# Two SBUF pools of a two-block transformer kernel taken from the other end of the memory

## The chip, the core and the metric

One NeuronCore of a Trainium2 chip runs the whole program in one launch. The metric is device time in microseconds (us): the median of the runs of a kernel. Engines are named as in the profile: PE is TensorE, PEld its weight loads, DVE is VectorE, ACT is ScalarE, POOL is GpSimd, SP the queue that issues most DMAs.

## What is computed

256 tokens of width 1024 pass through two float32 blocks. Cut to what matters:

```python
for l in range(2):                                   # first block
    x = x + 0.5 * swiglu(rms_norm(x, ffn1_norm[l]), ffn1_w1[l], ffn1_w2[l])
    x = x + hybrid_mixer(rms_norm(x, mix_norm[l]), ...)   # LRU, latent attention, convolution
    x = x + 0.5 * swiglu(rms_norm(x, ffn2_norm[l]), ffn2_w1[l], ffn2_w2[l])
x = rms_norm(x, final_norm)
h = x                                                # second block
h = h + dilated_mixer(rmsnorm(h, a_norm[0]), ...)    # three dilated attentions, merged
h = h + swiglu_2(rmsnorm(h, ffn_norm[0]), ...)
h = h + forgetting_mixer(rmsnorm(h, b_norm[0]), ...)
h = h + swiglu_2(rmsnorm(h, ffn_norm[1]), ...)
return rmsnorm(h, final_norm_2)
```

`swiglu(x, w1, w2)` is `(silu(g) * u) @ w2` with `g, u` the halves of `x @ w1`; the hidden width is 2816.

## The kernel before

Every large product is made of three reduced-precision (fp32r) products. An operand A is kept as two halves, AH (A rounded to fp32r) and AL (the rest), and A times W is AH·WH + AH·WL + AL·WH. So each tile product is three matmuls, lines 342, 343 and 344 in `tm` (tokens on the output partitions) or 359, 360 and 361 in `fm` (features on them).

In `tm` the activation half, 128x128, is the stationary operand, loaded before each matmul, and the weight half, 128x512 in most products, is the moving operand, streamed through. In `fm` it is the other way round, with 256 moving columns.

Weights come in slabs of 128x1024 float32 (`slab`, lines 323 to 325): SP loads one into a `raw` buffer, ACT rounds it to `H`, and DVE makes `L` by subtraction. There are five `raw` buffers, three `H` and three `L`, all in pool `wp`. Small long-lived tiles of the norms (sums of squares, scales, the scratch `scr`) are in pool `sp`.

Activation halves lie in different tiles. `XH`, `XL` (pool `xp`, with the residual `x`) hold the normed input of a stage; every first product of a stage reads them. The hidden halves `HH`, `HL` of the feed-forward layers, `XN`, `XP` (the input in two other token orders, dilated mixer), `OH`, `OL` (attention outputs), and in the hybrid mixer `fr`, `oH`, `oL`, `ycH`, `ycL` are in a pool that `scoped` opens for a stage and closes after it. The stages follow each other: feed-forward, hybrid mixer, feed-forward, twice; then dilated mixer, feed-forward, forgetting mixer, feed-forward.

The pools are stacked in the order in which they are opened, from the low end of each SBUF partition unless `side="right"` is given. Within a pool tiles follow each other, each padded to 32 bytes. The order of instructions on each engine, and what each waits for, comes from the recording order and a scheduler.

Of the kernel before, what the change touches and what calls it, by code (L numbers as in the profile page):

```python
# [19 lines left out]
S = 256  # L20
# [9 lines left out]
HD = 64  # L30
# [167 lines left out]
class K:  # L198
    def __init__(self, ctx, tc, A):
        self.ctx, self.tc, self.nc, self.A = ctx, tc, tc.nc, A  # L200
        self.n = 0
        P = lambda n, b=1, **k: ctx.enter_context(tc.tile_pool(name=n, bufs=b, **k))
        self.const = P("const")
        self.xp = P("xp")
        self.wp = P("wp", 3)
        self.sp = P("sp", 2)
        pp = P("pp", space=bass.MemoryType.PSUM)
        self.bank = pp.tile([128, 8, 512], F32, name="bank")
        self.psum("wide")
# [117 lines left out]
        return v(H), v(L)  # L327

    def tm(self, name, l, chunks, XH, XL):
        """Token-major products of several column chunks, their k-groups interleaved."""  # L330
        nc = self.nc
        ws = [WSPEC[name][1][c][1] for c in chunks]
        kt = WSPEC[name][0] // 128
        ps = [[self.mm()[:, :w] for _ in range(2)] for w in ws]
        for (k0, n), ci in itertools.product(_kgroups(name, ws[0]), range(len(chunks))):
            H, L = self.slab(name, l, chunks[ci], k0, n)
            for t in range(2):
                for k in range(n):
                    a, z = k0 + k == 0, k0 + k == kt - 1
                    xh, xl = (X[:, k0 + k, 128 * t:128 * t + 128] for X in (XH, XL))  # L340
                    p = ps[ci][t]
                    nc.tensor.matmul(p, xh, H[:, k, :], start=a, stop=False)  # L342
                    nc.tensor.matmul(p, xh, L[:, k, :], start=False, stop=False)  # L343
                    nc.tensor.matmul(p, xl, H[:, k, :], start=False, stop=z)  # L344
        return ps

    def fm(self, name, l, chunks, XH, XL):
        """Feature-major products of 256-column chunks, [128, 2, S] each, their k-groups interleaved."""
        nc = self.nc
        kt = WSPEC[name][0] // 128  # L350
        ps = [self.mm2() for _ in chunks]
        for k0, n in _kgroups(name, 256):
            for chunk, p in zip(chunks, ps):
                H, L = self.slab(name, l, chunk, k0, n)
                for k in range(n):
                    a, z = k0 + k == 0, k0 + k == kt - 1
                    for j in range(2):
                        wh, wl = H[:, k, 128 * j:128 * j + 128], L[:, k, 128 * j:128 * j + 128]
                        nc.tensor.matmul(p[:, j, :], wh, XH[:, k0 + k, :], start=a, stop=False)  # L359
                        nc.tensor.matmul(p[:, j, :], wl, XH[:, k0 + k, :], start=False, stop=False)  # L360
                        nc.tensor.matmul(p[:, j, :], wh, XL[:, k0 + k, :], start=False, stop=z)  # L361
        return ps

    def transpose_split(self, src, k0, n, OH, OL, ko, gain=None, const=None, dil=1):
        """Token-major src[:, t, columns] to feature-major halves OH/OL[:, ko.., :];
        the tokens by residue modulo dil first."""
        nc = self.nc
        for k in range(0, n, 2):
            m = min(2, n - k)
            p = self.pt()[:, :m * S].rearrange("p (k s) -> p k s", k=m)  # L370
            for j in range(m):
                for t in range(2):
                    nc.tensor.transpose(p[:, j, 128 * t:128 * t + 128],  # L373
                                        src[:, t, 128 * (k0 + k + j):128 * (k0 + k + j + 1)], self.ident)
            if gain is None:
                h, lo = OH[:, ko + k:ko + k + m, :], OL[:, ko + k:ko + k + m, :]
                if const is None:
                    nc.scalar.copy(h, p)
                    nc.vector.tensor_sub(lo, p, h.bitcast(F32))
                else:  # L380
                    nc.scalar.activation(h, p, AF.Copy, scale=const)
                    nc.vector.scalar_tensor_tensor(lo, p, const, h.bitcast(F32), op0=OP.mult, op1=OP.subtract)
            else:
                for j in range(m):
                    g = gain[:, ko + k + j:ko + k + j + 1]
                    h, lo, pj = OH[:, ko + k + j, :], OL[:, ko + k + j, :], p[:, j, :]
                    if dil > 1:
                        h, lo = (z.rearrange("p (c i) -> p c i", c=dil) for z in (h, lo))
                        pj = pj.rearrange("p (i c) -> p c i", c=dil)
                    nc.scalar.activation(h, pj, AF.Copy, scale=g)  # L390
                    nc.vector.scalar_tensor_tensor(lo, pj, g, h.bitcast(F32), op0=OP.mult, op1=OP.subtract)  # L391
# [31 lines left out]
        return r  # L423

    def norm_twice(self, row, g1, g2, dil):
        """x becomes its norm by g1; the operands and scales are those of the norm of that by g2,
        the operands' tokens by residue modulo dil first."""
        nc, x = self.nc, self.x
        es, p = self.scoped("twice")
        gb = p.tile([128, D], F32, name="gb")  # L430
# [66 lines left out]
        es.close()  # L497

    def log1p_exp(self, p, e, n, tag):
        """log(1 + e) for e in (0, 1], by 2 artanh(e / (2 + e))."""  # L500
        nc = self.nc
        z = p.tile([128, n], F32, name=tag + "z")
        z2 = p.tile([128, n], F32, name=tag + "y")
        q = p.tile([128, n], F32, name=tag + "q")
        nc.vector.tensor_scalar(z2, e, 2.0, None, op0=OP.add)
        nc.vector.reciprocal(z2, z2)
        nc.vector.tensor_mul(z, e, z2)
        nc.vector.tensor_mul(z2, z, z)
        nc.vector.tensor_scalar(q, z2, 1.0 / 17, None, op0=OP.mult)
        for c in (15, 13, 11, 9, 7, 5, 3):  # L510
            nc.vector.scalar_tensor_tensor(q, q, 1.0 / c, z2, op0=OP.add, op1=OP.mult)
        nc.vector.scalar_tensor_tensor(q, q, 1.0, z, op0=OP.add, op1=OP.mult)
        nc.vector.tensor_scalar(q, q, 2.0, None, op0=OP.mult)
        return q

    def rope(self, tmp, dst, src, n, c0, w):
        """Rotates the last-dim halves (w each) of src [128, 2, n, 2w] into dst."""
        nc = self.nc
        m = 2 * n * w
        tmp = [tmp[:, m * i:m * i + m].rearrange("p (t n w) -> p t n w", t=2, n=n) for i in range(4)]  # L520
        shape = [128, 2, n, w]
        cs = self.cos[:, :, None, c0:c0 + w].to_broadcast(shape)
        sn = self.sin[:, :, None, c0:c0 + w].to_broadcast(shape)
        x1, x2 = src[:, :, :, :w], src[:, :, :, w:2 * w]
        nc.vector.tensor_mul(tmp[0], x1, cs)
        nc.vector.tensor_mul(tmp[1], x2, sn)
        nc.vector.tensor_mul(tmp[2], x2, cs)
        nc.vector.tensor_mul(tmp[3], x1, sn)
        nc.vector.tensor_sub(dst[:, :, :, :w], tmp[0], tmp[1])
        nc.vector.tensor_add(dst[:, :, :, w:2 * w], tmp[2], tmp[3])  # L530

    def attend(self, ap, qk, mask, v, nm, den, o, act, local):
        """One head: qk holds its queries and keys, [w, 2 * S]; leaves P V in o[t] (PSUM).
        Blocks of scores: (queries 1, keys 0 | 1), (queries 0, keys 0), or only the diagonal ones;
        the causal mask leaves the first block as it is."""
        nc = self.nc
        n = 2 if local else 3
        keys = (0, 1) if local else (0, 1, 0)
# [24 lines left out]
                nc.tensor.matmul(o[t], PT[:, 128 * i:128 * i + 128], v[:, keys[i], :], start=i == a, stop=i == b - 1)  # L563

    def heads(self, ap, which, q, k, w, mask, v, store, act=False, local=False, stats=None):
        """Attention of heads a pair (from those of `which`) at a time; q, k: [128, 2, n, w] token-major, v: [128, 2, n, HD]."""
        nc = self.nc
        for h in which:
            ops = []
# [28 lines left out]
            store(h, o, nm, den)  # L598

    def normalized(self, ap, OH, OL, ko):  # L600
        """Keeps a pair of heads' normalized output as a feature tile of OH/OL."""
        nc = self.nc

        def store(h, o, nm, den):
# [5 lines left out]
        return store  # L610

    def bcast(self, dst, r):
        """Per-token column r [128, 2] to a row, the same on every partition."""
        nc = self.nc
        p = self.pt()[:, :S]
        for t in range(2):
# [305 lines left out]
    def dilated(self):  # L922
# [26 lines left out]
            nc.vector.tensor_scalar(one, r8[:, 2, 0:1], 1.0, 1.0, op0=OP.min, op1=OP.max)  # L949

        def copy(i, dst, src):
            """Scaled by one, which holds the copy back until the scales are there."""
            if i:
                nc.vector.tensor_scalar(dst, src, one, None, op0=OP.mult)
            else:
                nc.scalar.activation(dst, src, AF.Copy, scale=one)
# [179 lines left out]
```

## Time and profile before

| what | value |
|---|---|
| three runs, median (lowest to highest) | 2091.37 us (2090.86 to 2091.70) |
| span of the profiled execution | 2086.7 us |
| median of the runs less that span | 4.7 us |
| PE busy, of the span | 2052.3 us, 98% |
| chain that ended last, PE's share | 90% |
| DVE, ACT busy | 1304.4 us, 1088.6 us |
| DMA, mean over the span | 171 GB/s |

The profiled execution has no time of its own beside its span; what lies around the span is taken as the 4.7 us of the third row. A matmul's duration in the trace contains its way through the array and overlaps its neighbours, so how fast PE goes is read from the distance of two starts, not from durations.

### The profile page before, as it was taken

The numbers are of one execution on the slowest core, as the hardware profiler recorded it, in microseconds if no ns is written. First come the engines' busy times: TensorE is split into PE (matmuls) and PEld (weight loads), VectorE is DVE, ScalarE is ACT, GpSimd is POOL, SyncE is SP. The second block draws the span as 40 slices with busy tenths as digits, with TensorE's granted clock in tenths as the row PEclk, the third lists the DMA queues.
The fourth block names the chain that finished last, engine by engine and source line by source line (L and its number), as shares of the span: only waits on it lengthen the run. The fifth ranks groups of instructions, "written<-read, shape, count | busy, mean of one in ns | idle before, by whom it ended". The sixth has DMA issues, their size and how long they took to land.

```text
span 2086.7 us, 27788 instructions
## 1 busy us (share of the span) xinstructions
PE 2052.3 (98%) x10542; PEld 1709.8 (82%) x10542; DVE 1304.4 (63%) x2042; ACT 1088.6 (52%) x1681; POOL 19.7 (1%) x31
## 2 busy tenths in 40 slices
PE   8999999999999999999999999889999999999998
PEld 7888988788878888988788877667778888888886
DVE  4555999855555556998755565445775554555554
ACT  5444685554444445684554457445555544555443
POOL 0000000000000000000000000000000000000000
PEclk9999999999999999999999999999999999999999
DMA  6666554556565666454555554445436655436653
GB/s 218 183 204 193 180 172 153 171 185 185 181 188 181 190 179 201 158 181 152 191 182 184 181 171 137 141 145 177 131 111 183 187 179 160 130 103 192 183 181 120
DMA packets 100301, 356.00 MB, mean 171 GB/s; under 512 B 11176, under 2 KB 12216, under 8 KB 100168
## 3 DMA queue, kind: packets, MB, share of 16 engines
q1 hardware_dynamic: 98920, 351.69, 53.8%
q0 software_dynamic: 528, 1.26, 0.3%
q8 instruction: 82, 1.34, 0.3%
q10 hardware_dynamic: 720, 1.29, 0.2%
q14 instruction: 51, 0.42, 0.1%
HBM read 350.59 MB, written 3.21 MB: 170 GB/s over the span
## 4 chain that ended last, share of the span: by engine, by line
PE 90%; issue 3%; DMA 3%; ACT 2%; DVE 1%; POOL 0%; ACTq 0%; SPq 0%; POOLq 0%; DVEq 0%
PE bank L343 25%; PE bank L342 25%; PE bank L344 25%; PE bank L373 2%; PE bank L563 2%; PE bank L544 2%; PE bank L558 1%; PE bank L361 1%; PE bank L359 1%; PE bank L360 1%; DMA T<-X 1%; PE bank L584 1%; DVE L L325 1%; ACT H L324 1%; DMA x<-in_x 1%
## 5 line engine op out<-in xcount | busy, mean ns | idle before, releaser
L325 DVE TENSOR_TENSOR L<-raw,H 128x1024 fp32r<-128x1024 f32 (+1 forms) x653 | 791.9, 1214 | 628.3 <-ACT H L324 626.3
L324 ACT CAST H<-raw 128x1024 fp32r<-128x1024 f32 (+1 forms) x653 | 681.0, 1043 | 841.6 <-PE bank L344 782.4
L343 PE MATMUL bank<-L,XH 128*128 128x512 f32 (+3 forms) x1680 | 633.0, 377 | 6.7 <-DVE L L325 6.7
L342 PE MATMUL bank<-H,XH 128*128 128x512 f32 (+3 forms) x1680 | 638.0, 380 | 0.1
L344 PE MATMUL bank<-H,XL 128*128 128x512 f32 (+3 forms) x1680 | 629.5, 377 | 0.5 <-DVE XL L391 0.4
L343 PEld LDWEIGHTS bank<-L,XH 128*128 128x128 f32 x1680 | 318.3, 189 | 60.4 <-DVE L L325 8.3
L342 PEld LDWEIGHTS bank<-H,XH 128*128 128x128 f32 x1680 | 318.3, 189 | 55.3 <-ACT XH L390 2.0
L344 PEld LDWEIGHTS bank<-H,XL 128*128 128x128 f32 x1680 | 317.4, 189 | 56.2 <-DVE XL L391 2.6
L342 PE MATMUL bank<-H,HH 128*128 128x512 f32 x528 | 209.2, 396 | 0.0
L343 PE MATMUL bank<-L,HH 128*128 128x512 f32 x528 | 208.2, 394 | 0.0
L344 PE MATMUL bank<-H,HL 128*128 128x512 f32 x528 | 208.2, 394 | 0.0
L342 PEld LDWEIGHTS bank<-H,HH 128*128 128x128 f32 x528 | 99.2, 188 | 23.9
L344 PEld LDWEIGHTS bank<-H,HL 128*128 128x128 f32 x528 | 98.8, 187 | 24.2
L343 PEld LDWEIGHTS bank<-L,HH 128*128 128x128 f32 x528 | 98.9, 187 | 23.8
L787 DVE SCALAR_TENSOR_TENSOR acc<-cpad,cvec,acc 128x256 f32<-128x256 f32 x240 | 103.9, 476 | 0.0
L360 PE MATMUL bank<-XH,L 128*128 128x256 f32 x256 | 72.0, 283 | 0.0
L359 PE MATMUL bank<-XH,H 128*128 128x256 f32 x256 | 71.8, 285 | 0.1
L361 PE MATMUL bank<-XL,H 128*128 128x256 f32 x256 | 71.0, 284 | 0.1
L563 PEld LDWEIGHTS bank<-v,PT 128*128 128x128 f32 x416 | 54.0, 191 | 6.6 <-DVE PT L560 2.7
L563 PE MATMUL bank<-v,PT 128*128 128x64 f32 x416 | 55.3, 268 | 0.2 <-DVE PT L560 0.2
L486 DVE SCALAR_TENSOR_TENSOR h<-bank,r,t 128x512 f32<-128x512 f32 (+1 forms) x72 | 48.2, 699 | 8.3 <-PE bank L344 8.2
L485 ACT ACTIVATE t<-bank,r 128x512 f32<-128x512 f32 (+1 forms) x72 | 47.4, 659 | 10.1 <-PE bank L344 10.1
(329 smaller groups left out, 2178.7 us busy)
## 6 DMA issues: line engine op xcount, KB each, us to landing
raw<-in_ffn_w SPq DMA_DIRECT2D x264, 512.0 KB, 3.5
raw<-in_ffn_w_gu SPq DMA_DIRECT2D x88, 512.0 KB, 3.6
raw<-in_w_in SPq DMA_DIRECT2D x80, 512.0 KB, 3.5
raw<-in_a_w_in SPq DMA_DIRECT2D x72, 512.0 KB, 3.6
raw<-in_ffn_w_down SPq DMA_DIRECT2D x44, 512.0 KB, 3.6
raw<-in_b_w_in SPq DMA_DIRECT2D x24, 512.0 KB, 3.4
raw<-in_w_out SPq DMA_DIRECT2D x16, 512.0 KB, 3.5
raw<-in_mla_w_o SPq DMA_DIRECT2D x8, 512.0 KB
```

Of the source, the lines that this page charges most:

```text
L324: nc.scalar.copy(H[:, :nw], raw[:, :nw])
L325: nc.vector.tensor_sub(L[:, :nw], raw[:, :nw], H[:, :nw].bitcast(F32))
L342: nc.tensor.matmul(p, xh, H[:, k, :], start=a, stop=False)
L343: nc.tensor.matmul(p, xh, L[:, k, :], start=False, stop=False)
L344: nc.tensor.matmul(p, xl, H[:, k, :], start=False, stop=z)
L359: nc.tensor.matmul(p[:, j, :], wh, XH[:, k0 + k, :], start=a, stop=False)
L360: nc.tensor.matmul(p[:, j, :], wl, XH[:, k0 + k, :], start=False, stop=False)
L361: nc.tensor.matmul(p[:, j, :], wh, XL[:, k0 + k, :], start=False, stop=z)
L485: nc.scalar.activation(tt[:, t, :w], pg[t], AF.Silu, scale=r[:, t:t + 1])
L486: nc.vector.scalar_tensor_tensor(h[:, t, :w], pu[t], r[:, t:t + 1], tt[:, t, :w], op0=OP.mult, op1=OP.mult)
L563: nc.tensor.matmul(o[t], PT[:, 128 * i:128 * i + 128], v[:, keys[i], :], start=i == a, stop=i == b - 1)
L787: nc.vector.scalar_tensor_tensor(acc[:, c], cpad[:, c, tap:tap + S], dww[:, tap, c:c + 1], acc[:, c], op0=OP.mult, op1=OP.add)
```

## The change

The pools `wp` and `sp` are opened with `side="right"`, so they are stacked down from the high end of a partition. The pools of the stages, opened later at the low end, then begin where `XL` ends. The diff also blanks the docstrings of a dozen functions; these make no instruction.

```diff
         self.const = P("const")
         self.xp = P("xp")
-        self.wp = P("wp", 3)
-        self.sp = P("sp", 2)
+        self.wp = P("wp", 3, side="right")
+        self.sp = P("sp", 2, side="right")
         pp = P("pp", space=bass.MemoryType.PSUM)
...
     def tm(self, name, l, chunks, XH, XL):
-        """Token-major products of several column chunks, their k-groups interleaved."""
+
```

On all five engines the changed program has the same instructions in the same order, with the same waits, as the one before: no row of the order differs. All that differs is the place of tiles in a partition. Start addresses in bytes, from the two built programs, and what is left of them modulo 128:

| tile | before | mod 128 | after | mod 128 |
|---|---|---|---|---|
| `x`, `XH`, `XL` | 24064, 32256, 40448 | 0 | the same | 0 |
| `raw` (first of five, 4096 apart) | 48640 | 0 | 184288 | 96 |
| `H` (first of three, 4096 apart) | 69120 | 0 | 204768 | 96 |
| `L` (first of three, 4096 apart) | 81408 | 0 | 217056 | 96 |
| tiles of `sp` | 93696 to 96287 | | 181664 to 184255 | |
| start of a stage's pool | 96320 | 64 | 48640 | 0 |
| `HH`, `HL` (five of six layers) | 96320, 118848 | 64 | 48640, 71168 | 0 |
| `HH`, `HL` (last layer) | 108608, 131136 | 64 | 60928, 83456 | 0 |
| `XN0`, `XP0` | 112704, 129088 | 64 | 65024, 81408 | 0 |
| `fr`, `oH`, `ycH` | 122688, 168000, 184384 | 64 | 75008, 120320, 136704 | 0 |
| `OH` (dilated) | 96320 | 64 | 48640 | 0 |
| `OH`, `OL` (forgetting) | 96672, 104864 | 32 | 48992, 57184 | 96 |

Slices that a matmul reads of `XH`, `HH` and the like begin at multiples of 512 bytes in the tile, those of `H` and `L` in 512-column products at multiples of 2048, so the last column holds for each of them.

## Rows read from the trace of the kernel before

**Rows 1.** The page, parts 1 and 4: busy time by engine; chain that ended last.
```profile
PE 2052.3 (98%) x10542; PEld 1709.8 (82%) x10542; DVE 1304.4 (63%) x2042; ACT 1088.6 (52%) x1681; POOL 19.7 (1%) x31
...
PE 90%; issue 3%; DMA 3%; ACT 2%; DVE 1%; POOL 0%; ACTq 0%; SPq 0%; POOLq 0%; DVEq 0%
```

**Rows 2.** Instruction groups by shape, PE: line, out<-stationary pair, count | busy us, mean ns.
```profile
L342 PE MATMUL bank<-H,XH 128*128 128x512 f32 x1408 | 558.6, 397 | 0.1
...
L342 PE MATMUL bank<-H,HH 128*128 128x512 f32 x528 | 209.2, 396 | 0.0
...
L360 PE MATMUL bank<-XH,L 128*128 128x256 f32 x256 | 72.0, 283 | 0.0
...
L342 PE MATMUL bank<-H,XH 128*128 128x256 f32 x192 | 54.8, 285 | 0.0
...
L342 PE MATMUL bank<-H,XP 128*128 128x512 f32 x96 | 40.2, 419 | 0.0
...
L342 PE MATMUL bank<-H,XN 128*128 128x512 f32 x96 | 39.8, 414 | 0.0
...
L342 PE MATMUL bank<-H,OH 128*128 128x512 f32 x64 | 26.9, 420 | 0.2 <-ACT OH L378 0.2
...
L342 PE MATMUL bank<-H,fr 128*128 128x512 f32 x48 | 19.4, 404 | 0.0
...
L342 PE MATMUL bank<-H,ycH 128*128 128x512 f32 x32 | 12.8, 401 | 0.3 <-DVE ta L843 0.3
L342 PE MATMUL bank<-H,oH 128*128 128x512 f32 x32 | 12.7, 396 | 0.0
```

**Rows 3.** Timeline of PE (start us, duration us), feed-forward first product, stationary XH, XL.
```profile
439.80 0.39 PE L344 MATMUL bank<-H,XL 128*128 128x512 f32 x1
...
447.28 0.39 PE L344 MATMUL bank<-H,XL 128*128 128x512 f32 x1
```

**Rows 4.** The same view, feed-forward second product, stationary HH, HL.
```profile
760.15 0.39 PE L342 MATMUL bank<-H,HH 128*128 128x512 f32 x1
...
767.85 0.39 PE L342 MATMUL bank<-H,HH 128*128 128x512 f32 x1
```

**Rows 5.** The same view, forgetting mixer's output product, stationary OH, OL.
```profile
1878.73 0.39 PE L342 MATMUL bank<-H,OH 128*128 128x512 f32 x1
...
1886.43 0.39 PE L342 MATMUL bank<-H,OH 128*128 128x512 f32 x1
```

**Rows 6.** The same view, hybrid mixer, where the stationary operand changes from fr to XH.
```profile
357.32 0.39 PE L344 MATMUL bank<-H,fr 128*128 128x512 f32 x1
...
358.72 0.39 PE L344 MATMUL bank<-H,fr 128*128 128x512 f32 x1
358.95 0.39 PE L342 MATMUL bank<-H,XH 128*128 128x512 f32 x1
...
360.34 0.39 PE L342 MATMUL bank<-H,XH 128*128 128x512 f32 x1
...
361.70 0.39 PE L342 MATMUL bank<-H,XH 128*128 128x512 f32 x1
```

**Rows 7.** Instruction groups by shape, PEld and DVE, whole program.
```profile
L342 PEld LDWEIGHTS bank<-H,XH 128*128 128x128 f32 x1680 | 318.3, 189 | 55.3 <-ACT XH L390 2.0 <-ACT XH L381 0.4 <-ACT q L745 0.3
L342 PEld LDWEIGHTS bank<-H,HH 128*128 128x128 f32 x528 | 99.2, 188 | 23.9
...
L391 DVE SCALAR_TENSOR_TENSOR XL<-bank,cvec,XH 128x256 fp32r<-128x256 f32 x72 | 30.5, 476 | 0.9 <-ACT XH L390 0.5
L391 DVE SCALAR_TENSOR_TENSOR fr<-bank,cvec,fr 128x256 fp32r<-128x256 f32 x10 | 4.7, 475 | 0.0
```

**Rows 8.** Waits of the DMA queue SP: total us, times, longest.
```profile
SPq L323 <- DVE L L325: 1557.3, 593, 16.8
```

**Rows 9.** DMA issues: KB of each, median us to landing.
```profile
raw<-in_ffn_w SPq DMA_DIRECT2D x264, 512.0 KB, 3.5
```

## Prediction

> **What bounds the kernel.** I read the page first: PE is busy 98% of the span and 90% of the chain that ended last [rows 1]. So I look for what sets PE's pace. The view of groups by shape gives the counts of the 512-column products by the tile that is loaded as stationary operand. Line 342 has 1408 with `XH`, 528 with `HH`, 96 each with `XP` and `XN`, 64 with `OH`, 48 with `fr`, 32 each with `ycH` and `oH` [rows 2]. Lines 343 and 344 have as many, so there are 3 x 1408 = 4224 products with x's halves and 3 x 896 = 2688 with a stage's tiles.
>
> Durations there overlap, so the pace is read from starts in the timeline. With `XH` and `XL` loaded, a start at 439.80 and the 33rd after it at 447.28 us give 7.48 / 33 = 226.7 ns [rows 3]. With `HH` and `HL` it is 7.70 / 33 = 233.3 ns [rows 4], with the forgetting mixer's `OH` again 7.70 / 33 = 233.3 ns [rows 5]. The reader is to see that the same instruction, with the same shape and the same weight buffers, has two paces, 6.7 ns apart, by where its stationary operand lies. In these stretches PE waits for nothing.
>
> I counted all distances between 512-column products that follow each other; rows 3 to 6 are samples of them. With x's halves loaded 3519 are of 226 to 228 ns, 386 of 229 to 245, and 169 are longer (a stop). With a stage's tiles 2384 are of 229 to 245 ns, 22 shorter, 125 longer. The rest to 4224 and 2688 stand behind a transpose.
>
> **What sets the two paces.** In the table of addresses, x's halves lie below 48640 and a stage's tiles from 96320 up, so distance would explain it. So would alignment: x's halves and the weight buffers start at multiples of 128 bytes, all stage tiles 64 or 32 off. Two things speak against distance. A weight load lasts 189 ns from `XH` and 188 from `HH` [rows 7], so a far tile isn't read later. And the pace is a rhythm that falls into place: where the mixer goes from `fr` to `XH`, the last six distances with `fr` take 1.40 us (233 ns each), the first six with `XH` 1.39 us (232 ns), the next six 1.36 us (227 ns) [rows 6]. Nearness would help from the first matmul. A rhythm that settles looks like two streams, the moving operand and the next stationary one, that get in each other's way unless their addresses fit. They fit where both have the same remainder modulo 128. With a difference of 64 (`HH`) or 32 (the forgetting mixer's `OH`) they never settle. That is my reading; the trace doesn't show an address.
>
> **The change, part by part.** No instruction is added, removed or moved, and no wait. So every term is a change of pace.
>
> 1. *Products with x's halves.* `XH` stays at remainder 0, but `H` and `L` go to 96. The difference of stationary and moving operand becomes 32, the difference that the forgetting mixer's `OH` has now, at 233.3 ns [rows 5]. 3519 distances lose the fast pace: 3519 x 6.67 ns = +23.5 us. No row has a moving operand at such a place. From below I take 0 (only the stationary operand counts), from above the 4224 x 6.67 = 28.2 us of all [rows 2]. I take 23.5, by the row with the same difference.
>
> 2. *Products with a stage's tiles.* `HH`, `XN`, `XP`, `fr`, `oH`, `ycH` and the dilated `OH` go to remainder 0, but against `H` at 96 their difference is 32 too: they stay at 233.3 ns, so 0. If the stationary operand's own place decides, 2384 x 6.67 = -15.9 us, which is the lower end.
>
> 3. *The forgetting mixer's output.* `OH` goes to 96, the same as `H`: difference 0. Its 96 products (a part of the 64 x 3 with that name [rows 2]), less those behind a stop, gain 75 x 6.67 = -0.5 us.
>
> 4. *Narrower products.* 256 columns: 3 x 256 in `fm` and 3 x 192 in `tm` [rows 2], 1344 in all. Their pace at other differences isn't in the trace. One step of 6.67 ns for each would be +9.0 us, none is 0. I take 0, and 9 for the upper end.
>
> 5. *ACT, DVE, DMA.* DVE's split of 128x256 takes 476 ns into `XL` and 475 into `fr` [rows 7], at remainders 0 and 64, near and far, so its time doesn't hang on the place, and I cost it at 0. The weights' DMAs land in 3.5 us, and SP waits 1557 us in all for a `raw` buffer to be read by DVE [rows 8, 9]. Loads run ahead of use by up to five buffers; if each took a tenth longer, 0.35 us, this cover would hide it. If the cover were gone, PE would wait at line 343 for `L`.
>
> Sum, from the profiled span of 2086.7 us: + 23.5 - 0.5 = 2109.7 us. The median of the three runs lies 4.7 us above the span, so I forecast **2114.4 us**, 23 us or 1.1% slower than 2091.37. This case's own range is 2106 (a third of the products keep the fast pace, 1173 x 6.67 = 7.8 us less) to 2124 (all narrow products lose a step too: 2114.4 + 9.0).
>
> **A rule against this reading.** The rows show 226.7 and 233.3 ns for one instruction at two places [rows 3, 4]. The Trainium skill, "SBUF — State Buffer", section "Who interferes with whom", gives TensorE two read ports of its own, one for each operand, and says that it never waits on anyone. By that rule addresses would be free and the time would stay at 2091.4. The trace speaks against it, unless something beside the address sets the two paces; it is the third rival.
>
> **Rivals.**
>
> *A: the stationary operand's own place decides, faster.* Either nearness or its own remainder of 0 brings the fast pace, and the weights' place doesn't matter. Then term 1 is 0 and term 2 counts, less the forgetting mixer: 2384 - 75 = 2309 distances x 6.67 = 15.4 us, 2091.4 - 15.4 = **2076.0 us**. For it: all fast products lie low and are at remainder 0, all others neither. It also needs that moving operands far up or 96 off cost nothing, and no row shows one. Against it: the settling in [rows 6] and equal weight loads in [rows 7]. It shows from 630 products on that reach 227 ns while those with `XH` keep it (630 x 6.67 ns = 4.2 us).
>
> *B: both operands must be near.* Weights at the far end cost a step in every 512-column product, the stage's tiles gain theirs: `XH` goes to 233.3 ns, `HH` stays. The sum is that of my forecast by another mechanism, so it is in the same chance; the forgetting mixer's 0.5 us alone would tell them apart.
>
> *C: addresses aren't it.* The tiles of a stage differ from x's halves in something that the change leaves alone, or gain and loss cancel. Then 2091.4 us, as the rule above has it. For it: I have no row with the same tile at two places. Against it: `HH`, `XN`, `fr` and `OH` come from different stages with different work beside them, and share only where they lie.
>
> **Chances.** Forecast (with B) 0.55, A 0.32, C 0.13. Differences within 0.2% (4.2 us) are about what a measurement of this kernel can't tell from none: its three runs lie within 0.9 us. So faster 0.32, same 0.13, slower 0.55. Cases of both signs hold most of the chance, so the range goes from A to the upper end of the forecast, 2075 to 2124; the forecast's own is 2106 to 2124.
>
> **What would show it.** Right: in the timeline after, 33 distances with `XH` take 7.70 us instead of 7.48 in every feed-forward layer, those with `HH` still 7.70, those of the forgetting mixer's output 7.48, and DVE's and ACT's means are unchanged. A would show 7.48 for both `XH` and `HH`, with the gain in the second products of the six feed-forward layers: 1584 x 6.67 = 10.6 us of it. A mixed picture, with `XH` slower by more than one step, would put the time above 2124 and make the alignment of the moving operand a cost of its own. Weight loads that PE waits for at line 343 would mean that DMAs to the new places are slow, which none of these foresees.

## The result, and the profile after

The change makes the kernel slower: 2111.01 us, the median of four runs (2109.82 to 2113.42), against 2091.34 us for the kernel before (four runs, 2090.86 to 2091.70). The ratio is 1.0098, with a 95% interval of 1.0084 to 1.0113. The forecast was 2114.4 us, with 2106 to 2124 as its case's own range, and 2075 to 2124 with its rivals. The mean granted clock of TensorE was 0.993 in the profiled execution before and 0.992 after, and in the stretches shown below it was 1.00 (the 2.4 GHz level), so the paces in them aren't set by the clock.

The page of the changed kernel: busy time by engine, the costliest DVE group and the largest group of the weights' DMAs.

```profile
span 2109.6 us, 27788 instructions
...
PE 2074.0 (98%) x10542; PEld 1708.6 (81%) x10542; DVE 1305.3 (62%) x2042; ACT 1089.1 (52%) x1681; POOL 19.7 (1%) x31
...
L325 DVE TENSOR_TENSOR L<-raw,H 128x1024 fp32r<-128x1024 f32 (+1 forms) x653 | 792.3, 1214 | 650.8 <-ACT H L324 649.0
...
raw<-in_ffn_w SPq DMA_DIRECT2D x264, 512.0 KB, 3.5
```

The same DVE group on the page of the kernel before:

```profile
L325 DVE TENSOR_TENSOR L<-raw,H 128x1024 fp32r<-128x1024 f32 (+1 forms) x653 | 791.9, 1214 | 628.3 <-ACT H L324 626.3
```

PE's busy time grew from 2052.3 [rows 1] to 2074.0 us, 21.7 of the 22.9 us by which the span grew. DVE and ACT stay within 1 us, and a slab still lands in 3.5 us [rows 9]. So the time went into PE's pace, and its place is seen in the timeline. Each pair below is a start and the 33rd start after it, as in rows 3 to 5; I call the time from one start to the next a distance. The columns are start, duration (us), engine, line and tiles. The timeline of PE after shows the first and the second product of a feed-forward layer and the forgetting mixer's output product:

```profile
444.72 0.40 PE L343 MATMUL bank<-L,XH 128*128 128x512 f32 x1
...
452.42 0.40 PE L343 MATMUL bank<-L,XH 128*128 128x512 f32 x1
...
776.63 0.40 PE L342 MATMUL bank<-H,HH 128*128 128x512 f32 x1
...
784.33 0.40 PE L342 MATMUL bank<-H,HH 128*128 128x512 f32 x1
...
1898.79 0.39 PE L342 MATMUL bank<-H,OH 128*128 128x512 f32 x1
...
1906.46 0.39 PE L342 MATMUL bank<-H,OH 128*128 128x512 f32 x1
```

With `XH` 33 distances take 7.70 us where they took 7.48 [rows 3]: 233.3 ns each, not 226.7. With `HH` in the second product they still take 7.70 [rows 4]. With `OH` of the forgetting mixer, the third pair, they take 7.67 us where they took 7.70 [rows 5].

At the step from `fr` to `XH` in the hybrid mixer, after:

```profile
362.87 0.40 PE L344 MATMUL bank<-H,fr 128*128 128x512 f32 x1
363.11 0.40 PE L342 MATMUL bank<-H,XH 128*128 128x512 f32 x1
...
364.51 0.40 PE L342 MATMUL bank<-H,XH 128*128 128x512 f32 x1
...
365.91 0.40 PE L342 MATMUL bank<-H,XH 128*128 128x512 f32 x1
```

The first six distances with `XH` take 1.40 us, 233 ns each, and so do the next six: nothing settles as it did in [rows 6].

One thing is faster. In `fm`, with 256 moving columns, I compare a sample of 66 distances. Before:

```profile
211.81 0.28 PE L361 MATMUL bank<-XL,H 128*128 128x256 f32 x1
...
219.72 0.28 PE L361 MATMUL bank<-XL,H 128*128 128x256 f32 x1
```

After:

```profile
215.74 0.28 PE L361 MATMUL bank<-XL,H 128*128 128x256 f32 x1
...
223.44 0.28 PE L361 MATMUL bank<-XL,H 128*128 128x256 f32 x1
```

That is 7.91 us before and 7.70 after, or 119.8 and 116.7 ns each.

I counted every distance between neighbouring 512-column products again, as in the prediction. Of those with x's halves loaded, 3519 were of at most 228 ns; now 13 are.

### The profile page after: what moved, and what is told of

The parts are those of the page before. It is cut to its first block, busy times and chain, and to the rows that moved or that the text cites. A ratio compares the mean times of both kernels' runs of the same rounds, so it can differ in the third digit from the quotient of the medians.

```text
span 2109.6 us, 27788 instructions
## 1 busy us (share of the span) xinstructions
PE 2074.0 (98%) x10542; PEld 1708.6 (81%) x10542; DVE 1305.3 (62%) x2042; ACT 1089.1 (52%) x1681; POOL 19.7 (1%) x31
## 4 chain that ended last, share of the span: by engine, by line
PE 87%; issue 4%; DVE 4%; DMA 3%; ACT 2%; POOL 0%; ACTq 0%; SPq 0%; POOLq 0%; DVEq 0%
PE bank L343 25%; PE bank L342 25%; PE bank L344 25%; PE bank L373 2%; PE bank L563 2%; PE bank L544 2%; PE bank L558 1%; DMA T<-X 1%; DVE L L325 1%; PE bank L584 1%; ACT H L324 1%; DVE acc L787 1%; PE bank L361 1%; PE bank L360 1%; PE bank L359 1%
## 5 line engine op out<-in xcount | busy, mean ns | idle before, releaser
L325 DVE TENSOR_TENSOR L<-raw,H 128x1024 fp32r<-128x1024 f32 (+1 forms) x653 | 792.3, 1214 | 650.8 <-ACT H L324 649.0
L343 PE MATMUL bank<-L,XH 128*128 128x512 f32 (+3 forms) x1680 | 641.2, 382 | 6.1 <-DVE L L325 6.1
L342 PE MATMUL bank<-H,XH 128*128 128x512 f32 (+3 forms) x1680 | 645.8, 384 | 0.1
L344 PE MATMUL bank<-H,XL 128*128 128x512 f32 (+3 forms) x1680 | 637.4, 381 | 0.5 <-DVE XL L391 0.4
```

The source lines that it names most:

```text
L325: nc.vector.tensor_sub(L[:, :nw], raw[:, :nw], H[:, :nw].bitcast(F32))
```

## The experiments

The theory of the forecast is that the pace of a product hangs on the difference of the start addresses of its two operands, and that they fit (reach the fast pace) where this is a multiple of 128 bytes. Against it stand: that the weights' far end costs by itself; that the stationary operand's own place decides; that the place in absolute terms matters, not the difference; and another modulus than 128. Each experiment only shifts tiles, by a pad that nothing writes or reads or by one pool's side.

| run | stationary less moving, modulo 256: `XH`; `HH` | time, median (range), us | ratio to before [95%] |
|---|---|---|---|
| before | 0; 64 | 2091.34 | |
| after | 32; 32 | 2111.01 (2109.82 to 2113.42) | 1.0098 [1.0084, 1.0113] |
| e1_stage_to_128 | 0; 128 | 2088.79 (2087.55 to 2090.48) | 0.999 [0.998, 0.9999] |
| e1b_stage_to_512 | 0; 0 | 2077.24 (2076.55 to 2077.94) | 0.9933 [0.9919, 0.9948] |
| e2_far_to_128 | 128; 128 | 2110.22 (2108.21 to 2111.34) | 1.0093 [1.0076, 1.0110] |
| e2b_far_to_512 | 0; 0 | 2077.10 (2076.83 to 2077.30) | 0.9933 [0.9918, 0.9947] |
| e3_all_by_64 | 0; 0 | 2078.92 (2078.59 to 2079.25) | 0.9944 [0.9928, 0.9961] |
| e4_all_by_32 | 0; 0 | 2078.19 (2077.58 to 2079.11) | 0.9941 [0.9926, 0.9956] |
| e5_small_right | 0; 0 | 2078.11 (2076.37 to 2079.21) | 0.9939 [0.9925, 0.9954] |
| e6_weights_right | 32; 96 | 2113.15 (2111.84 to 2114.07) | 1.0107 [1.0092, 1.0122] |
| e7_forget_too | 0; 0 | 2076.92 (2076.20 to 2078.13) | 0.9934 [0.9921, 0.9948] |

The kernel before took 2090.40 to 2091.56 us (medians) beside the experiments.

### The stage's tiles moved, the weights left where they were

The kernel before with a pad in `sp`, so that a stage's pool starts at 96384 instead of 96320, a multiple of 128:

```diff
-        self.sp = P("sp", 2)
+        self.sp = P("sp", 2); self.sp.tile([128, 16], F32, name="pad", bufs=1)
```

> The kernel before, with 64 unused bytes at the end of the pool of small tiles: a stage's tiles begin at 96384, a multiple of 128 (128 modulo 512), instead of 96320; weights stay at 69120 and 81408. Theory P (both operands of a 512-column product must start at multiples of 128 for the fast pace): products with HH, XN, fr, oH go from 233.3 to 226.7 ns, about 2309 x 6.67 ns = 15 us less, 2076 us. Theory P512 (multiples of 512 are needed, or a difference of 0 modulo 512): HH stays at 233.3 ns, 2091 us. Theory N (both operands must lie near the low end): 2091 us.

The second product of a feed-forward layer in its timeline, 33 distances:

```profile
751.76 0.39 PE L343 MATMUL bank<-L,HH 128*128 128x512 f32 x1
...
759.43 0.40 PE L343 MATMUL bank<-L,HH 128*128 128x512 f32 x1
```

7.67 us, 232.4 ns each: one nanosecond less than at 64, and not the fast pace. The time falls by 2.5 us, where the forecast's rule wanted 15. So 128 is not the modulus. Next the same with a longer pad, `[128, 112]`, so that the pool starts at 96768, a multiple of 512:

> The kernel before, with 448 unused bytes at the end of the pool of small tiles: a stage's tiles begin at 96768, a multiple of 512. Theories P and P512: HH at 226.7 ns, about 2076 us (by P512 fr, at 256 modulo 512, stays at 233.3 ns and it is 1 us more). Theory N: HH is as far as before, 233.3 ns, 2091 us.

```profile
352.20 0.39 PE L342 MATMUL bank<-H,fr 128*128 128x512 f32 x1
...
356.96 0.39 PE L342 MATMUL bank<-H,fr 128*128 128x512 f32 x1
...
749.83 0.40 PE L342 MATMUL bank<-H,HH 128*128 128x512 f32 x1
...
757.32 0.39 PE L342 MATMUL bank<-H,HH 128*128 128x512 f32 x1
```

With `HH` (second pair) 33 distances take 7.49 us, 227.0 ns each. `fr` lies 26368 bytes into the pool, so it starts at 256 modulo 512, and its 21 distances (first pair) take 4.76 us, 226.7 ns each. The modulus is therefore 256, not 512. Of the distances with a stage's tiles other than `OH`, 2039 are now of at most 228 ns, where 20 were. The gain is 2091.25 - 2077.24 = 14.0 us, and 2019 x 6.7 ns = 13.5 us.

### The weights shifted at the far end

The changed kernel with a pad of 96 bytes under the right-hand pools, so that `H` and `L` go from 224 to 128 modulo 256:

```diff
-        self.xp = P("xp")
+        self.xp = P("xp"); P("rpad", side="right").tile([128, 24], F32, name="pad")
```

> The changed kernel, with 96 unused bytes at the very end of the partition: H at 204672 and L at 216960, multiples of 128 (384 modulo 512), as far as in the changed kernel; stage tiles stay at 48640. Theory P: all products of 512 columns but those with the forgetting mixer's OH at 226.7 ns, 2091 - 15 = 2076 us. Theory P512: still 233.3 ns, 2111 us. Theory N (far weights cost a step): 2111 us.

First product of a feed-forward layer:

```profile
442.34 0.39 PE L342 MATMUL bank<-H,XH 128*128 128x512 f32 x1
...
450.00 0.40 PE L342 MATMUL bank<-H,XH 128*128 128x512 f32 x1
```

7.66 us, 232.1 ns: again nearly the slow pace at a difference of 128, and 2110.22 us where the forecast's rule wanted 2076. The pad made 480 bytes long (`[128, 120]`) puts `H` at 204288 and `L` at 216576, both multiples of 256, still at the far end:

> The changed kernel, with 480 unused bytes at the very end of the partition: H at 204288 and L at 216576, multiples of 512, still at the far end. Theories P and P512: 226.7 ns with XH and HH, 2076 us. Theory N: 233.3 ns, 2111 us.

```profile
436.50 0.39 PE L342 MATMUL bank<-H,XH 128*128 128x512 f32 x1
...
443.99 0.39 PE L342 MATMUL bank<-H,XH 128*128 128x512 f32 x1
...
573.44 0.39 PE L342 MATMUL bank<-H,HH 128*128 128x512 f32 x1
...
580.92 0.39 PE L342 MATMUL bank<-H,HH 128*128 128x512 f32 x1
```

7.49 us with `XH`, 7.48 with `HH`. The weights lie as far away as in the changed kernel, and both products are fast: 2077.10 us. So the far end costs nothing here, which ends rival B. These 384 bytes of pad more than in the run before it are worth 33 us.

### Everything off alignment by the same amount

Here the kernel before gets a pad in `const` as well, so that x's halves, the weights and the stage's tiles all start at 64 modulo 256:

```diff
-        self.const = P("const")
+        self.const = P("const"); self.const.tile([128, 16], F32, name="pad")
...
-        self.sp = P("sp", 2)
+        self.sp = P("sp", 2); self.sp.tile([128, 48], F32, name="pad", bufs=1)
```

> The kernel before with x's halves, weights and stage tiles all at 64 modulo 256 (64 unused bytes in the first pool, 192 in that of small tiles); every difference of stationary and moving operand is 0 modulo 256. Theory D (the difference decides): 226.7 ns with XH and with HH, 2077 us. Theory M (each operand must be at a multiple of 256 itself): 233 ns everywhere, about 3519 x 6.67 ns = 23 us above before, 2114 us.

```profile
437.58 0.39 PE L342 MATMUL bank<-H,XH 128*128 128x512 f32 x1
...
445.06 0.39 PE L342 MATMUL bank<-H,XH 128*128 128x512 f32 x1
...
751.63 0.39 PE L342 MATMUL bank<-H,HH 128*128 128x512 f32 x1
...
759.11 0.39 PE L342 MATMUL bank<-H,HH 128*128 128x512 f32 x1
```

Both take 7.48 us. The same with `[128, 8]` in `const`, everything at 32 modulo 256:

> As e3_all_by_64, with everything at 32 modulo 256, so that no operand starts at a multiple of 64. Theory D: 226.7 ns with XH and with HH, 2077 us. Theory M: 233 ns everywhere, 2114 us. A third, D64 (the difference decides, and each must be at a multiple of 64): 2077 us for e3_all_by_64 and 2114 us here.

```profile
438.58 0.39 PE L342 MATMUL bank<-H,XH 128*128 128x512 f32 x1
...
446.06 0.39 PE L342 MATMUL bank<-H,XH 128*128 128x512 f32 x1
...
782.37 0.39 PE L344 MATMUL bank<-H,HL 128*128 128x512 f32 x1
...
789.85 0.39 PE L344 MATMUL bank<-H,HL 128*128 128x512 f32 x1
```

With x's halves and with the hidden halves (second pair) 33 distances take 7.48 us, and the time is 2078.19 us. Both operands may start 64 or 32 bytes off, if they do so together: only the difference counts. The last section has the same for products that don't fit.

### The two halves of the change, one at a time

First only the small tiles' pool at the far end, and the weights left where they were. A stage's pool then starts at 93696, a multiple of 256:

```diff
-        self.sp = P("sp", 2)
+        self.sp = P("sp", 2, side="right")
```

> One half of the change alone: only the pool of small tiles goes to the far end. Stage tiles begin at 93696, a multiple of 256, weights stay at multiples of 256. Theories D and M: 226.7 ns with XH and HH, 2077 us, better than both kernels. A theory in which the far end itself costs: 2091 us or more.

It takes 2078.11 us. `XH` and `HH` both take 7.48 us for 33 distances, while `OH` of the forgetting mixer, 96 modulo 256 here, does not:

```profile
1869.81 0.40 PE L342 MATMUL bank<-H,OH 128*128 128x512 f32 x1
...
1877.55 0.40 PE L342 MATMUL bank<-H,OH 128*128 128x512 f32 x1
```

7.74 us, 234.5 ns. Then only the weights' pool:

```diff
-        self.wp = P("wp", 3)
+        self.wp = P("wp", 3, side="right")
```

> The other half alone: only the pool of the weights goes to the far end, where H and L start at 224 modulo 256; stage tiles begin at 51264, 64 modulo 256. Differences are 32 for XH and 96 for HH. Theories D and M: 233 ns with both, the whole loss of the change, 2111 us.

```profile
444.04 0.40 PE L342 MATMUL bank<-H,XH 128*128 128x512 f32 x1
...
451.74 0.40 PE L342 MATMUL bank<-H,XH 128*128 128x512 f32 x1
...
613.15 0.40 PE L342 MATMUL bank<-H,HH 128*128 128x512 f32 x1
...
620.89 0.39 PE L342 MATMUL bank<-H,HH 128*128 128x512 f32 x1
```

7.70 us with `XH`, as in the whole change, and 7.74 with `HH` at a difference of 96. It takes 2113.15 us. So the loss comes from the weights' half of the change alone. The other half gains 12.3 us by itself, and in the whole change that gain is lost, because the weights then lie at 224 and a stage's tiles at 0.

### A version faster than both

The gain of e5_small_right, with the forgetting mixer's `OH` moved by 160 bytes to 94208, a multiple of 256:

```diff
-        OH = p.tile([128, 8, S], F32R, name="OH")
+        p.tile([128, 40], F32, name="pad"); OH = p.tile([128, 8, S], F32R, name="OH")
```

> e5_small_right with 160 unused bytes ahead of the forgetting mixer's OH and OL, which then start at multiples of 256 as well, so that every 512-column product has a difference of 0 modulo 256. Theory D: 33 distances in that output product take 7.48 us instead of 7.70; some 70 distances x 6.67 ns = 0.5 us below e5_small_right, 2077.5 us, which the interval can't tell from it. Theory M the same.

```profile
1870.14 0.39 PE L343 MATMUL bank<-L,OH 128*128 128x512 f32 x1
...
1877.62 0.39 PE L343 MATMUL bank<-L,OH 128*128 128x512 f32 x1
```

7.48 us, 226.7 ns. The count of distances of at most 228 ns with an `OH` or `OL` loaded goes from 27 to 70, worth 43 x 7.8 ns = 0.3 us, which the time can't tell: 2076.92 against 2078.11 us, on different chips and each beside other runs of the kernel before. The version's ratio to the kernel before is 0.9934 [0.9921, 0.9948], 0.7% faster, but it isn't told apart from e1b_stage_to_512 or e2b_far_to_512.

## Why the prediction was right, and where it was not

*What bounds the kernel* was right. PE's pace set the end: its busy time moved by 21.7 us, the span by 22.9, DVE's and ACT's busy time by less than 1.

*Term 1, products with x's halves, +23.5 us:* right. 3506 fast distances were lost (3519 to 13), 3506 x 6.67 ns = 23.4 us. The guess that a moving operand at this place costs what the row with the same remainder modulo 128 showed [rows 5] held to within the reading. That was luck in part: modulo 256 that row's difference is 160 and the new one is 32, so they weren't the same case, and only happen to share 233.3 ns. The difference of 192, also a misfit, gives 229 (last section).

*Term 2, a stage's tiles, 0:* right, 7.70 us for 33 distances as in [rows 4].

*Term 3, the forgetting mixer's output, -0.5 us:* wrong, and here the step "they fit where both have the same remainder modulo 128" failed. The difference is 128 there, and 33 distances take 7.67 us, not 7.48. The modulus is 256, which e1_stage_to_128 and e2_far_to_128 show on two other tiles. It cost the forecast little only because no more than 75 distances had that difference. The same rule, used on e2_far_to_128, missed by 34 us.

*Term 4, narrower products, 0 to +9 us:* the sign was wrong. Counted over all distances without a stop, the mean in `fm` went from 119.9 to 117.0 ns, 768 x 2.9 = 2.2 us (the sample above has 3.1 ns). In `tm` the counted mean of 256-column products went from 119.9 to 118.2 ns, 576 x 1.7 = 1.0 us. I had bounded the term from below by 0 with no reason that excludes a gain. I had also left out the 336- and 384-column products; they kept their paces (154 and 174 ns before and after).

*Term 5, DVE, ACT and DMA, 0:* right. DVE's line 325 takes 1214 ns on average at the old places and at the new ones, and a slab lands in 3.5 us as before [rows 9].

The measured terms give 23.4 - 0.1 - 3.2 = 20.1 us (0.1 for `OH`, 75 x 0.9 ns), and the medians differ by 2111.01 - 2091.34 = 19.7. The forecast had 23.0, and the missed term 4 makes up most of the 3.3 us between them. The spans differ by 22.9 instead, but they are two single executions. In the profiled run of after, 1.7 us lie around the span (2111.33 - 2109.6), and 1.8 in those of the nine experiments, so the 4.7 us that the forecast took for it are too many: if as much lies around it before, the profiled execution of before was 3 us below its median. The traces bear this out. Compared start by start, after takes 2.6 us more than before at stops and where one kind of product follows another, and the nine experiments take 1.2 to 4.5 us more there, whichever way their tiles lie. So the trace of before is short at its stops, and 2.6 of the 22.9 us aren't the change's pace.

*Rival A* (the stationary operand's own place, 0.32) is refuted by the result: `XH` didn't move and lost its pace. Its 2076 us turned up all the same in e1b, e2b and e5, by the forecast's mechanism with 256 for 128. *Rival B* falls by e2b_far_to_512, and *C* by the result itself.

*The rule against this reading.* The Trainium skill, "SBUF — State Buffer", section "Who interferes with whom", lists two independent read ports for TensorE. The runs do not agree that addresses are therefore free: the same instructions in the same order took 2077.10 us and 2110.22 us with the weights' buffers 384 bytes apart. What the two reads share isn't seen in any trace. That they are the moving operand's and the next weight load's is inferred from the settling in [rows 6] and from the pace depending on the difference alone, and stays an inference.

## What to carry to other kernels

Where PE is busy nearly all the time with 512-column fp32r products that each load new weights, let both operands of a product start at addresses that differ by a multiple of 256 bytes, whatever these addresses are. As tiles start at multiples of 32 bytes here, a pad of at most 224 bytes does it; in this kernel the fit was worth 0.7%, while losing it cost 1%. The 256-column products went the other way, by less (3.2 us gained where those of 512 columns lost 23.4). So after any edit of pools, print the addresses: a change that issues the same instructions isn't neutral, and a small tile added to a low pool shifts all pools behind it. And read PE's pace from starts in the timeline, by the tile that is loaded; the groups' mean durations show two paces only dimly.

## What the runs showed that I had not expected

- The slow pace has shades by the difference of the two starts modulo 256: 232.1 to 232.5 ns at 128, 233.3 at 32, 64 and 160 (the last is `OH` in [rows 5]), 234.5 at 96 (`OH` in e5, `HH` in e6), against 226.7 to 227.0 at 0. A misfit isn't always this slow: in e6_weights_right the forgetting mixer's `OH` lies at 160 and `H` at 224, a difference of 192, and 33 distances take 7.56 us, 229 ns:

```profile
1899.72 0.39 PE L344 MATMUL bank<-H,OL 128*128 128x512 f32 x1
...
1907.28 0.39 PE L344 MATMUL bank<-H,OL 128*128 128x512 f32 x1
```

  A difference of 192 is 64 the other way, and yet not as slow as 64 itself; no other run has it. The shades too go by the difference and not by the places. The same 51 distances with this `OH` or `OL` have a mean of 234.3 ns in e1b_stage_to_512, with `OH` at 96 and `H` at 0, and in e3_all_by_64, with `OH` at 160 and `H` at 64: both have 96. They have 233.3 in e1_stage_to_128 (224 and 0) and in e2_far_to_128 (96 and 128): both have 224. Counted over the 2216 distances of 231 to 245 ns with a stage's tiles other than `OH`, the mean is 234.3 ns in e6_weights_right and 233.4 after: 2.0 us, about the 2.1 us between the two times, which their intervals can't tell apart.
- The 256-column products in `fm` go the other way. Their mean duration, line 360, shows it by run. Before, and in e2_far_to_128 (difference 128):

```profile
L360 PE MATMUL bank<-XH,L 128*128 128x256 f32 x256 | 71.8, 283 | 0.0
```

  and after:

```profile
L360 PE MATMUL bank<-XH,L 128*128 128x256 f32 x256 | 70.9, 279 | 0.0
```

  The row is that of e2_far_to_128; before has 283 ns too [rows 2]. In e6_weights_right, with `H` and `L` at 224 as after, it is 280 ns, and at a difference of 0 it is 283 or 284. So the 3 ns come with the weights at 224 modulo 256, and x's halves at 0. Why shorter products gain where longer ones lose is open. So is whether a kernel could have both: no run put the weights of `fm` and of `tm` at different remainders.
- A fit that is lost for a moment isn't found again at once. In e5_small_right, where all these operands fit, 271 distances with x's halves and 190 with a stage's tiles are still of 231 to 245 ns. Of these 461, 452 are among the first twelve after a stop or after another kind of product, 9 come later. So nearly all stand where [rows 6] shows the pace settling, and at 6.7 ns each they cost 3.1 us: after each interruption, up to a dozen fitting products go at the slow pace.
